# Scaling x by the FFN norm's factor on VectorE, and a new order of a pair's seven products, in a two-layer decoder trunk on one core

## The chip, the cores and the metric

The kernel runs on one core of one Trainium2 chip. The metric is device time in microseconds (us) for one execution; smaller is better. The median of three runs of the kernel before is 954.46 us (953.52 to 955.66).

## The reference

Two layers, 256 tokens, width 1024, float32. Each layer is an FFN, a token mixer (layer 0 stick-breaking attention, layer 1 latent attention), and another FFN, so there are four FFNs. Each of these is wrapped in a norm before and a norm after.

```python
def rms_norm(x, g):
    y = x * lax.rsqrt(jnp.mean(x * x, axis=-1, keepdims=True) + EPS)
    return y * g
def swiglu(x, w_in, w_out):
    gate, up = jnp.split(x @ w_in, 2, axis=-1)
    return (jax.nn.silu(gate) * up) @ w_out
...
f = swiglu(rms_norm(x, g[0]), ffn_w_in[i, 0], ffn_w_out[i, 0])
x = x + 0.5 * rms_norm(f, g[1])
```

## The kernel before, in words

The 256 tokens are two blocks of 128 (one token per partition). Every float32 product is made of three matmuls of a high and a low part: a weight piece (128 rows by 512 columns) is loaded, ScalarE rounds it to the high part (`split`, L368), VectorE subtracts to get the low part (L375), and TensorE runs hi*hi, hi*lo, lo*hi (`mm3`, L545). The pieces form one fixed stream. All operations are put in a list and a planner (`Plan.run`, L185) orders each engine's instructions ahead of time from assumed durations; an operation of class 0 goes ahead of the stream's work (class 1), and if a class 0 operation will be ready within `HOLD` us, the engine is left idle for it. On the chip each engine then runs its instructions strictly in that order.

**The norm ahead of an FFN** (`pre_norm`, L621, with `scaled=True`): for a block, ScalarE squares and sums the two halves of x (L609), VectorE adds the sums and eps into the mean square `msx` (L611, one number per token), GpSimd raises it to -0.5 with `half_neg` into `rpre` (L613), ScalarE scales the two halves of x by `rpre` (L634), TensorE transposes them in blocks of 128 (L551, 4 to a half), VectorE multiplies by the gain out of PSUM (L641). The result is split into high and low parts (L561 or L567, and L581), and these are the FFN's operands. This is done for both blocks, one after the other, while TensorE works on what it can.

**A pair** is 512 columns of gate and of up for both blocks at once, by seven 512-wide products in place of eight (`pair_product`, L769): the weights' quarters "11", "12", "21", "22" are combined by sums (`add_pair`, L416), some on VectorE (L434), some by a DMA that GpSimd issues and that adds on arrival (L437; which of them, `SUMS` tells). Each product is 4 pieces, so 12 matmuls. `STEPS` names the products in order: products 1, 6, 7 and 4 accumulate in one PSUM bank Z, 5 and 3 in a bank W, 2 in a bank Y. After products 1, 5 and 6 ScalarE copies the bank as it then stands to SBUF (`keep`, L759); the next product in the same bank can't write before the copy has been made. After 6 VectorE forms `up0` = W - m6 (L762), and then the hidden values of block 0.

`FFN_ORDERS` sets the order of the FFN's work: `s0.3` is the fourth product of pair 0, `i2` a plain tile of 256 columns, `o` and `t` rows of the second weight matrix. There are three pairs (s0, s1, s2). In pair 0 the products `s0.4` and `s0.5` follow one another directly; with `STEPS` = "1253674" these are 6 and 7.

Of the kernel before, what the change touches and what calls it, by code (L numbers as in the profile page):

```python
# [39 lines left out]
NEG = -(2.0 ** 100)  # L40


LEADS = [14, 12, 13, 17, 13, 7]
CAPS = [28, 27, 24, 26, 25, 26]
RESERVE = [4, 6, 2, 4, 3, 6]
AHEAD = 8
# [1 line left out]
ADD_US = 8.0  # L48
RSLOTS = 66
WSLOTS = 27  # L50
HOLD = 0.26
STOCK = 6
X1_AT = 1
WARM_A = 4
# [2 lines left out]


PAIR = 512
STEPS = "1253674"  # L60
SUMS = ["4", "124", "1"]
FFN_ORDERS = [
    ("s0.0 i0 i1 s0.1 s0.2 o0 o1 s0.3 s0.4 s0.5 i2 s0.6 s1.0 t0.0 s1.1 s1.2 t0.1 t0.2 s1.3 s1.4 i3 t0.3 s1.5 "
     "o2 s1.6 s2.0 s2.1 t1.0 t1.1 s2.2 t1.2 s2.3 s2.4 o3 s2.5 t1.3 s2.6 t2.0 i4 t2.1 t2.2 t2.3 o4"),
] * 4

# [40 lines left out]


class Op:
    __slots__ = ("eng", "us", "fn", "cls", "deps", "users", "wait", "bufs", "ready", "end", "table", "blk", "piece", "alt", "phase", "debt", "first", "lat", "size")  # L110


class Plan:
# [12 lines left out]
    def op(self, eng, us, fn, r=(), w=(), cls=0, after=(), table=None, blk=None, piece=None):  # L126
        o = Op()
        o.eng, o.us, o.fn, o.cls, o.table, o.blk, o.piece = eng, us, fn, cls, table, blk, piece
        o.alt = {}
        deps = set(after)  # L130
        bufs = {}
        for b, p in r:
            deps.update(b.wr.get(p, ()))
            b.rd.setdefault(p, []).append(o)
            bufs[id(b)] = b
        for b, p in w:
            deps.update(b.wr.get(p, ()))
            deps.update(b.rd.get(p, ()))
            b.wr[p] = [o]
            b.rd[p] = []  # L140
            bufs[id(b)] = b
        deps.discard(o)
        o.deps = list(deps)
        o.users = []
        o.wait = len(o.deps)
        o.bufs = list(bufs.values())
        o.ready, o.end = 0.0, None
        o.debt = 0
        o.first = None
        o.lat = 2.0 if eng == "dma" else 0.0  # L150
        o.size = 0
        for b in o.bufs:
            b.left += 1
        for d in o.deps:
            d.users.append(o)
        self.ops.append(o)
        return o
# [27 lines left out]
    def run(self):  # L185
        engines = ("pe", "act", "dve", "pool", "dma")
        at = dict.fromkeys(engines, 0.0)
        known = {e: [] for e in engines}

        def know(o):  # L190
            for e in (o.eng, *o.alt):
                known[e].append(o)

        for o in self.ops:
            if o.wait == 0:
                know(o)
        table = None
        left = len(self.ops)
        while left:
            best = None  # L200
            for e in engines:
                if not known[e]:
                    continue
                cand = []
                for o in known[e]:
                    if o.first is not None and (
                            o.first - self.split_pos >= AHEAD or
                            len(self.free["w"]) < KEEP):
                        continue
                    if o.debt > 0 and (self.held >= CAPS[o.phase] or  # L210
                                       len(self.free["r"]) - self.debt < 2 + RESERVE[o.phase]):
                        continue
                    cand.append((max(o.ready, self.slots_ready(o), self.bank_ready(o, e), at[e]), o))
                if not cand:
                    continue
                t = min(c[0] for c in cand)
                if t < math.inf and (best is None or t < best[0]):
                    best = (t, e, cand)
            assert best is not None, (at, self.held, self.pos, self.split_pos,
                                      {e: [(o.ready, o.cls, [b.tag for b in o.bufs]) for o in k[:6]] for e, k in known.items()},  # L220
                                      {t_: len(f) for t_, f in self.free.items()})
            t, e, cand = best
            now = [(o.cls, w, o) for w, o in cand if w <= t]
            if e == "pe":
                side = [c for c in now if c[0] == 0]
                if side:
                    o = min(side, key=lambda c: c[1])[2]
                else:
                    lead = self.pos[0] - self.pos[1]
                    by = {c[2].blk[0]: c[2] for c in now}  # L230
                    o = by[0] if 0 in by and (1 not in by or lead < LEADS[by[0].phase]) else by[1]
            else:
                o = min(now, key=lambda c: (c[0], c[1]))[2]
                if o.cls > 0 and (o.piece is None or self.split_pos - self.pos[0] >= STOCK):
                    soon = [w for w, q in cand if q.cls == 0 and t < w < t + HOLD]
                    if soon:
                        at[e] = min(soon)
                        continue
            us, fn = (o.us, o.fn) if e == o.eng else o.alt[e]
            if o.table is not None and o.table != table:  # L240
                self.set_table(o.table)
                table = o.table
                us += 1.3
            for b in o.bufs:
                if b.tile is None:
                    f = self.free[b.tag]
                    s_ = min(x for x in f)
                    f.remove(s_)
                    b.slot = s_[1]
                    b.tile = self.tiles[b.tag][b.slot]  # L250
            fn()
            at[e] = t + us
            o.end = t + us + o.lat
            if o.size:
                at["dma"] = max(at["dma"], t) + o.size / 180e3
            if o.piece is not None:
                if e == "act":
                    self.held += 1
                    self.split_pos = o.piece + 1
                elif e == "pe":  # L260
                    for q in o.blk:
                        self.pos[q] = o.piece + 1
                    if 1 in o.blk:
                        self.held -= 1
            self.debt += o.debt
            for b in o.bufs:
                b.touch[e] = o.end
                b.left -= 1
                b.end = max(b.end, o.end)
                if b.left == 0 and b.slot is not None:  # L270
                    self.free[b.tag].append((b.end + CROSS, b.slot))
            for q in (o.eng, *o.alt):
                known[q].remove(o)
            left -= 1
            for u in o.users:
                u.ready = max(u.ready, at[e] if u.eng == e and not u.alt else o.end + CROSS)
                u.wait -= 1
                if u.wait == 0:
                    know(u)
        return max(at.values())  # L280
# [11 lines left out]
def trunk(ctx: ExitStack, tc: tile.TileContext, x, positions, norm_g, ffn_w_in, ffn_w_out,  # L292
# [313 lines left out]
    def rstd(srcs, ss, ms, r, scale, eps, cls=0):  # L606

        for h, (src, rd) in enumerate(srcs):
            op("act", act_us(512, 1), lambda src=src, h=h: nc.scalar.activation(  # L609
                junk[:], src(), AF.Square, scale=scale, accum_out=ss[:, h:h + 1]), r=rd, w=[(ss, h)], cls=cls)  # L610
        op("dve", 0.13, lambda: nc.vector.tensor_scalar(ms[:], ss[:, 0:1], ss[:, 1:2], eps, op0=ALU.add, op1=ALU.add),  # L611
           r=[(ss, 0), (ss, 1)], w=[(ms, 0)])
        op("pool", 0.46, lambda: nc.gpsimd.tensor_tensor(out=r[:], in0=ms[:], in1=half_neg[:], op=ALU.pow),  # L613
           r=[(ms, 0)], w=[(r, 0)])

    def stats(b, cls):
        k = blocks[b]
        rstd([(lambda h=h: xt[b][h][:], [(xt[b][h], 0)]) for h in range(2)], k.ss2, k.ms2, k.rpre,
             1.0 / math.sqrt(D), EPS, cls)

    def pre_norm(b, l, i, scaled=False):  # L621

# [1 line left out]
        k = blocks[b]  # L624
        gi = (l * 6 + i) * KC
        k.xh, k.xl, k.y = [Buf("r"), Buf("r")], [Buf("r"), Buf("r")], [Buf("w"), Buf("w")]
        if scaled:
            stats(b, 0)
        for h in range(2):
            y, tr = k.y[h], Buf("bank")  # L630
            xs = xt[b][h]
            if scaled:
                xs = Buf("w")
                op("act", act_us(512, 1), lambda h=h, xs=xs: nc.scalar.activation(  # L634
                    xs[:], xt[b][h][:], AF.Copy, scale=k.rpre[:]), r=[(xt[b][h], 0), (k.rpre, 0)], w=[(xs, 0)])

            def turn(xs=xs, tr=tr):
                for c in range(4):
# [130 lines left out]
    def pair_product(l, f, p, step, st):  # L769
# [18 lines left out]
            vec512(st[nm], o, st[x], how)  # L788
        if q in "156":
            keep("m" + q)  # L790
            if q == "6":
                st["up0"] = Buf("w")
                vec512(st["up0"], st["W"], st["m6"], ALU.subtract)
                pair_hidden(0, p, st["gate0"], 1.0, st["up0"])
        elif q == "2":
            combine("gate0", "m1", ALU.add)
        elif q == "7":
            combine("up1", "m5", ALU.subtract)
        elif q == "4":
            pair_hidden(1, p, o, -1.0, st["up1"])  # L800

    def pair_hidden(b, p, gate, sign, up):
        h, hid = Buf("w"), Buf("w")
# [541 lines left out]
```

## Time and profile before

| | |
|---|---|
| runs, median of 3 | 954.46 us |
| the profiled execution, its own time | 953.05 us |
| its span, first to last instruction | 951.3 us |
| mean granted TensorE clock | 0.997 |
| ScalarE busy | 663.5 us (70%) |
| GpSimd busy | 104.3 us (11%) |

The span is what the views divide; 1.75 us of the execution's own time lie around it. Engines are PE (TensorE), PEld (its weight loads), DVE (VectorE), ACT (ScalarE), POOL (GpSimd). A wait is idle time of an engine just before an instruction, put down to the instruction that ended it.

### The profile page before, as it was taken

How to read it: one execution, taken by the hardware profiler on the slowest of the kernel's cores; microseconds unless marked ns; L12 is line 12 of the kernel's file. 1: busy time of each engine (PE TensorE's matmuls, PEld its weight loads, DVE VectorE, ACT ScalarE, POOL GpSimd, SP SyncE). 2: the span in 40 equal slices, each digit the busy share in tenths (PEclk: the TensorE clock that was granted, in tenths of full speed). 3: DMA queues.
4: the chain of work that ended last, by engine and by line, in shares of the span. 5: the costliest groups of instructions: out<-in, count | busy, mean ns of one | idle time of the engine just before them, and what ended most of it. 6: DMA issues, size and time to landing. Idle time of an engine off the chain costs nothing. (4 is left out here: it accounts for less than half of the span.)

```text
span 951.3 us, 14520 instructions
## 1 busy us (share of the span) xinstructions
PE 927.6 (98%) x4431; PEld 769.5 (81%) x4431; DVE 816.4 (86%) x1495; ACT 663.5 (70%) x1368; POOL 104.3 (11%) x155
## 2 busy tenths in 40 slices
PE   6999999999999899999999999999999999999997
PEld 4878888888888787888887878888898888788885
DVE  6999889877788898889978988797799999879982
ACT  8856767558798775767676666674689967576751
POOL 2013010000000112210001121100201000221000
PEclk9999999999999999999999999999999999999999
DMA  9799979834453369996933899778233255999731
GB/s 308 245 262 268 291 223 300 271 122 134 135 173 113 107 209 247 271 290 217 355 98 115 217 274 302 221 240 283 80 101 102 65 188 178 259 251 296 243 114 45
DMA packets 132462, 195.34 MB, mean 205 GB/s; under 512 B 12224, under 2 KB 63776, under 8 KB 132384
## 3 DMA queue, kind: packets, MB, share of 16 engines
q1 hardware_dynamic: 120752, 173.39, 54.9%
q0 software_dynamic: 11520, 20.98, 13.3%
q8 instruction: 35, 0.57, 0.2%
q14 instruction: 43, 0.35, 0.1%
q10 hardware_dynamic: 112, 0.05, 0.0%
HBM read 193.32 MB, written 1.05 MB: 204 GB/s over the span
## 5 line engine op out<-in xcount | busy, mean ns | idle before, releaser
L543 PE MATMUL bank<-r,r 128*128 128x512 f32 (+4 forms) x3936 | 890.1, 383 | 4.3 <-ACT w L759 3.4
L543 PEld LDWEIGHTS bank<-r,r 128*128 128x128 f32 (+1 forms) x3936 | 711.0, 188 | 141.4 <-ACT w L759 5.1
L375 DVE TENSOR_TENSOR r<-w,r 128x512 fp32r<-128x512 f32 (+2 forms) x772 | 485.7, 681 | 25.7 <-ACT r L368 20.9
L368 ACT CAST r<-w 128x512 fp32r<-128x512 f32 (+2 forms) x772 | 428.1, 617 | 79.1 <-DVE w L434 38.5
L437 POOL DMA_DIRECT2D w<-in_ffn_w_in_dram x80 | 70.9, 1140 | 339.9 <-DVE r L375 197.2
L561 ACT CAST r<-bank 128x256 fp32r<-128x256 f32 (+5 forms) x142 | 60.3, 440 | 44.6 <-PE bank L551 38.1
L581 DVE TENSOR_TENSOR r<-bank,r 128x256 fp32r<-128x256 f32 (+5 forms) x142 | 70.3, 503 | 15.6 <-ACT r L561 13.7
L434 DVE TENSOR_TENSOR w<-w,w 128x512 f32<-128x512 f32 x112 | 72.9, 683 | 0.0
L551 PE MATMUL bank<-ident,w 128*128 128x128 f32 (+1 forms) x390 | 62.3, 280 | 10.3 <-ACT w L634 9.3
L551 PEld LDWEIGHTS bank<-ident,w 128*128 128x128 f32 (+1 forms) x390 | 48.1, 140 | 26.5 <-ACT w L634 12.5
L715 ACT ACTIVATE w<-bank 128x256 f32<-128x256 f32 x40 | 15.3, 382 | 53.0 <-PE bank L543 52.9
L613 POOL TENSOR_TENSOR rpost<-ms,half_neg 128x1 f32<-128x1 f32 x12 | 6.6, 551 | 392.7 <-DVE ms L611 392.7
L759 ACT COPY w<-bank 128x512 f32<-128x512 f32 x36 | 21.1, 586 | 24.7 <-PE bank L543 24.2
L717 DVE TENSOR_TENSOR w<-bank,w 128x256 f32<-128x256 f32 x40 | 16.9, 421 | 23.0 <-ACT w L715 22.3
L762 DVE TENSOR_TENSOR w<-bank,w 128x512 f32<-128x512 f32 x36 | 24.8, 689 | 12.0 <-ACT w L759 7.8
L581 DVE TENSOR_TENSOR r<-w,r 128x512 fp32r<-128x512 f32 x48 | 32.4, 686 | 1.4 <-ACT r L576 0.4
L609 ACT ACTIVATE junk<-bank 128x512 bf16<-128x512 f32 x24 | 14.3, 596 | 18.3 <-PE bank L543 17.9
L660 DVE TENSOR_TENSOR w<-bank,w 128x512 f32<-128x512 f32 x24 | 16.4, 684 | 11.7 <-ACT junk L609 11.4
L762 DVE TENSOR_TENSOR w<-w,w 128x512 f32<-128x512 f32 x24 | 16.6, 692 | 8.8 <-ACT w L766 8.3
L641 DVE TENSOR_TENSOR w<-bank,gT 128x512 f32<-128x512 f32 x24 | 16.2, 685 | 5.7 <-PE bank L551 5.4
L766 ACT ACTIVATE w<-bank 128x512 f32<-128x512 f32 x12 | 7.2, 598 | 16.6 <-PE bank L543 10.3
L613 POOL TENSOR_TENSOR rpre<-msx,half_neg 128x1 f32<-128x1 f32 x12 | 13.5, 1122 | 45.0 <-DVE msx L611 32.0
(97 smaller groups left out, 331.7 us busy)
## 6 DMA issues: line engine op xcount, KB each, us to landing
w<-in_ffn_w_in_dram SPq DMA_DIRECT2D x368, 256.0 KB, 4.8
w<-in_ffn_w_out_dram SPq DMA_DIRECT2D x176, 256.0 KB, 5.2
w<-in_ffn_w_in_dram POOLq DMA_DIRECT2D x80, 256.0 KB, 7.4
w<-in_sb_w_in_dram SPq DMA_DIRECT2D x48, 256.0 KB, 5.2
w<-in_sb_w_out_dram SPq DMA_DIRECT2D x16, 256.0 KB, 3.6
w<-in_mla_w_out_dram SPq DMA_DIRECT2D x16, 256.0 KB, 3.1
w<-in_norm_g_dram SPq DMA_DIRECT2D x12, 256.0 KB, 4.2
w<-in_mla_w_in_dram SPq DMA_DIRECT2D x8, 208.0 KB, 4.7
```

The costliest lines, as they stand in the source:

```text
L368: h = op("act", act_us(n), lambda: nc.scalar.copy(pc.hi[:, :n], raw[:, :n]), r=[(raw, 0)], w=[(pc.hi, 0)], cls=1, after=splits[-1:], piece=i)
L375: nc.vector.tensor_tensor(out=pc.lo[:, :n], in0=raw[:, :n], in1=pc.hi[:, :n].bitcast(F32), op=ALU.subtract)
L434: op("dve", dve_us(PAIR), lambda d=d, t=t: nc.vector.tensor_add(out=d[:], in0=d[:], in1=t[:]), r=[(d, 0), (t, 0)], w=[(d, 0)], cls=1)
L437: o = op("pool", 0.9, lambda d=d, k=k: nc.gpsimd.dma_start(d[:], source(src, k), accum_op=ALU.add), r=[(d, 0)], w=[(d, 0)], cls=1)
L543: nc.tensor.matmul(o, a, b, start=start, stop=stop, skip_group_check=True)
L551: nc.tensor.transpose(o, i, ident[:])
L561: nc.scalar.copy(dst(), src())
L581: nc.vector.tensor_tensor(out=dst(), in0=src(), in1=hi().bitcast(F32), op=ALU.subtract)
L613: op("pool", 0.46, lambda: nc.gpsimd.tensor_tensor(out=r[:], in0=ms[:], in1=half_neg[:], op=ALU.pow), r=[(ms, 0)], w=[(r, 0)])
L717: op("dve", dve_us(FT), lambda: nc.vector.tensor_mul(out=hid[:, FT:], in0=o[:, FT:], in1=hid[:, 0:FT]), r=[(o, 0), (hid, 0)], w=[(hid, 1)])
L759: op("act", act_us(512), lambda: nc.scalar.copy(dst[:], src[:]), r=r, w=w)
L762: op("dve", dve_us(512), lambda: nc.vector.tensor_tensor(out=dst[:], in0=x[:], in1=y[:], op=o), r=[(x, 0), (y, 0)], w=[(dst, 0)])
```

## The change

The scaling of x by `rpre` moves from ScalarE to VectorE. Through a new field `then` of an operation the planner lets VectorE take nothing else between `msx` and the first scaling, nor between the first and the second. The products of a pair are made in the order 1, 2, 5, 6, 3, 7, 4; `up0` and what follows from it are made when 2, 3 and 6 are all done. In `FFN_ORDERS` the piece `t0.1` moves ahead of the second pair's second product. `HOLD` goes from 0.26 to 0.116, and one entry of `LEADS` (by how many pieces block 0 may be ahead of block 1, here in the second FFN) from 13 to 14.

```diff
-LEADS = [14, 12, 13, 17, 13, 7]
+LEADS = [14, 12, 14, 17, 13, 7]
...
-HOLD = 0.26
+HOLD = 0.116
...
-STEPS = "1253674"
+STEPS = "1256374"
...
-    ("s0.0 i0 i1 s0.1 s0.2 o0 o1 s0.3 s0.4 s0.5 i2 s0.6 s1.0 t0.0 s1.1 s1.2 t0.1 t0.2 s1.3 s1.4 i3 t0.3 s1.5 "
+    ("s0.0 i0 i1 s0.1 s0.2 o0 o1 s0.3 s0.4 s0.5 i2 s0.6 s1.0 t0.0 t0.1 s1.1 s1.2 t0.2 s1.3 s1.4 i3 t0.3 s1.5 "
...
+        only = {}
...
                 for o in known[e]:
+                    if only.get(e) not in (None, o):
+                        continue
...
             fn()
+            only[e] = o.then
...
-        if scaled:
-            stats(b, 0)
+        prev = stats(b, 0) if scaled else None
...
-                op("act", act_us(512, 1), lambda h=h, xs=xs: nc.scalar.activation(
-                    xs[:], xt[b][h][:], AF.Copy, scale=k.rpre[:]), r=[(xt[b][h], 0), (k.rpre, 0)], w=[(xs, 0)])
+                prev.then = op("dve", dve_fast_us(512) + 0.06, lambda h=h, xs=xs: nc.vector.tensor_scalar(
+                    xs[:], xt[b][h][:], k.rpre[:], None, op0=ALU.mult), r=[(xt[b][h], 0), (k.rpre, 0)], w=[(xs, 0)])
+                prev = prev.then
...
             keep("m" + q)
-            if q == "6":
-                st["up0"] = Buf("w")
-                vec512(st["up0"], st["W"], st["m6"], ALU.subtract)
-                pair_hidden(0, p, st["gate0"], 1.0, st["up0"])
...
+        done = STEPS[:step + 1]
+        if q in "236" and all(c in done for c in "236"):
+            st["up0"] = Buf("w")
+            vec512(st["up0"], st["W"], st["m6"], ALU.subtract)
+            pair_hidden(0, p, st["gate0"], 1.0, st["up0"])
```

VectorE in the third FFN, second block, before (w, r are SBUF buffers, x_193 the block's x; line 375 is a low part of the stream):

```order
L663 SCALAR_TENSOR_TENSOR x_193<-w_133,rpost_205,x_193 128x512
L434 TENSOR_TENSOR w_148<-w_148,w_136 128x512
L375 TENSOR_TENSOR r_110<-w_137,r_123 128x512
L611 TENSOR_SCALAR msx_207<-ssx_206 128x1
L375 TENSOR_TENSOR r_75<-w_134,r_105 128x512
L375 TENSOR_TENSOR r_63<-w_135,r_109 128x512
L375 TENSOR_TENSOR r_94<-w_141,r_111 128x512
L375 TENSOR_TENSOR r_96<-w_145,r_113 128x512
L375 TENSOR_TENSOR r_114<-w_153,r_68 128x512
L641 TENSOR_TENSOR w_137<-bank_158,gT 128x512
L641 TENSOR_TENSOR w_134<-bank_159,gT 128x512
```

The same place of the change, where lines stand 5 to 8 lower (L641 is now the scaling, L649 the gain, L439 a weight sum, L380 the low part):

```order
L671 SCALAR_TENSOR_TENSOR x_193<-w_145,rpost_205,x_193 128x512
L439 TENSOR_TENSOR w_135<-w_135,w_150 128x512
L380 TENSOR_TENSOR r_117<-w_128,r_104 128x512
L616 TENSOR_SCALAR msx_207<-ssx_206 128x1
L641 TENSOR_SCALAR w_144<-x_193,rpre_208 128x512
L641 TENSOR_SCALAR w_136<-x_193,rpre_208 128x512
L439 TENSOR_TENSOR w_131<-w_131,w_137 128x512
L649 TENSOR_TENSOR w_146<-bank_157,gT 128x512
L649 TENSOR_TENSOR w_153<-bank_160,gT 128x512
```

Five low parts stood between mean square and gain; now the two scalings and one weight sum stand there.

TensorE in the first FFN, pair 0, before: the last matmuls of product 6 and the first of product 7 (bank_160 is Z):

```order
L543 MATMUL bank_160<-r_107,r_103 128x512
L543 MATMUL bank_160<-r_84,r_103 128x512
L543 MATMUL bank_160<-r_107,r_120 128x512
L543 MATMUL bank_160<-r_109,r_88 128x512
L543 MATMUL bank_160<-r_87,r_88 128x512
L543 MATMUL bank_160<-r_109,r_102 128x512
```

The change, at the end of product 6:

```order
L548 MATMUL bank_160<-r_99,r_112 128x512
L548 MATMUL bank_160<-r_105,r_112 128x512
L548 MATMUL bank_160<-r_99,r_125 128x512
L548 MATMUL bank_156<-r_101,r_126 128x512
L548 MATMUL bank_156<-r_107,r_126 128x512
L548 MATMUL bank_156<-r_101,r_88 128x512
```

Product 3 in the other bank (bank_156, W) now follows product 6; product 7 comes 12 matmuls later.

## Rows read from the trace of the kernel before

**Rows 1.** The page's part 1: busy us of each engine, share of the span, instructions.
```profile
PE 927.6 (98%) x4431; PEld 769.5 (81%) x4431; DVE 816.4 (86%) x1495; ACT 663.5 (70%) x1368; POOL 104.3 (11%) x155
```

**Rows 2.** Waits of PE: line waited for, us in total, times, longest us.
```profile
PE bank L551 <- ACT w L634: 9.3, 4, 3.9
PE bank L543 <- ACT w L759: 3.4, 4, 1.3
PE bank L543 <- DVE r L375: 0.7, 2, 0.5
```

**Rows 3.** Timeline, third FFN, second block: start us, us, engine, line, form, count [idle before].
```profile
502.84 0.20 DVE L611 TENSOR_SCALAR msx<-ssx 128x1 f32<-128x1 f32 x1
502.96 3.09 DVE L375 TENSOR_TENSOR r<-w,r 128x512 fp32r<-128x512 f32 x5
503.19 3.27 POOL L613 TENSOR_TENSOR rpre<-msx,half_neg 128x1 f32<-128x1 f32 x1 [2.92 <-DVE msx L611]
507.27 1.62 PE L551 MATMUL bank<-ident,w 128*128 128x128 f32 x8 [2.10 <-ACT w L634]
507.96 0.69 DVE L641 TENSOR_TENSOR w<-bank,gT 128x512 f32<-128x512 f32 x1 [1.91 <-PE bank L551]
508.54 5.02 PE L543 MATMUL bank<-r,r 128*128 128x512 f32 x15
```

**Rows 4.** Timeline, second FFN: first block's factor, then the second block.
```profile
307.99 0.55 POOL L613 TENSOR_TENSOR rpre<-msx,half_neg 128x1 f32<-128x1 f32 x1 [3.81 <-DVE msx L611]
320.46 3.27 POOL L613 TENSOR_TENSOR rpre<-msx,half_neg 128x1 f32<-128x1 f32 x1 [2.92 <-DVE msx L611]
324.54 1.27 PE L551 MATMUL bank<-ident,w 128*128 128x128 f32 x8 [2.41 <-ACT w L634]
325.23 1.30 DVE L641 TENSOR_TENSOR w<-bank,gT 128x512 f32<-128x512 f32 x2 [1.91 <-PE bank L551]
325.56 2.77 PE L543 MATMUL bank<-r,r 128*128 128x512 f32 x11
```

**Rows 5.** Windows in the third FFN: us, PE busy, PEclk, DMA share, GB/s.
```profile
508.50:510.00 1.50, 1.50 (x6) 0.50 0.04 8
510.00:512.00 2.00, 2.00 (x7) 0.64 0.40 125
```

**Rows 6.** Timeline of the program's start, first block, and PE's first wait on VectorE.
```profile
5.77 0.56 POOL L613 TENSOR_TENSOR rpre<-msx,half_neg 128x1 f32<-128x1 f32 x1 [2.12 <-DVE msx L611]
7.52 0.72 ACT L634 ACTIVATE w<-x,rpre 128x512 f32<-128x512 f32 x1
8.29 1.12 PE L551 MATMUL bank<-ident,w 128*128 128x128 f32 x4 [3.93 <-ACT w L634]
9.45 0.69 DVE L641 TENSOR_TENSOR w<-bank,gT 128x512 f32<-128x512 f32 x1 [1.11 <-PE bank L551]
16.14 0.96 PE L543 MATMUL bank<-r,r 128*128 128x512 f32 x3 [0.49 <-DVE r L375]
```

**Rows 7.** Line L759 (copies of products): who waited, us and times.
```profile
  PE bank L543: 3.4, 4
```

**Rows 8.** VectorE's groups by shape: busy us, mean ns, idle before.
```profile
L375 DVE TENSOR_TENSOR r<-w,r 128x512 fp32r<-128x512 f32 x756 | 477.8, 683 | 25.7 <-ACT r L368 20.9 <-issue 1.8 <-PE bank L543 1.4
L567 DVE CAST r<-w 128x512 fp32r<-128x512 f32 x7 | 3.0, 427 | 0.2
L583 DVE SCALAR_TENSOR_TENSOR r<-bank,rpre,r 128x512 fp32r<-128x512 f32 x4 | 3.0, 748 | 0.1
```

**Rows 9.** Timeline, fourth FFN, second block.
```profile
770.21 3.09 DVE L375 TENSOR_TENSOR r<-w,r 128x512 fp32r<-128x512 f32 x5
770.43 0.86 POOL L613 TENSOR_TENSOR rpre<-msx,half_neg 128x1 f32<-128x1 f32 x1 [3.08 <-DVE msx L611]
```

**Rows 10.** Line L437 (accumulating DMAs), from issue to landing.
```profile
DMA to landing us min/median/max: 3.9/7.4/11.4
```

**Rows 11.** Chain that ended last, one long piece of PE: start us, us, count.
```profile
571.37 23.17 PE bank L543 x102
```

More of the change, by code (lines that the diff above doesn't have):

```diff
@@ L109 @@
 class Op:
-    __slots__ = ("eng", "us", "fn", "cls", "deps", "users", "wait", "bufs", "ready", "end", "table", "blk", "piece", "alt", "phase", "debt", "first", "lat", "size")
+    __slots__ = ("eng", "us", "fn", "cls", "deps", "users", "wait", "bufs", "ready", "end", "table", "blk", "piece", "alt", "phase", "debt", "first", "lat", "size", "then")
 class Plan:
@@ L151, in op @@
         o.size = 0
+        o.then = None
         for b in o.bufs:
@@ L610, in rstd @@
                 junk[:], src(), AF.Square, scale=scale, accum_out=ss[:, h:h + 1]), r=rd, w=[(ss, h)], cls=cls)
-        op("dve", 0.13, lambda: nc.vector.tensor_scalar(ms[:], ss[:, 0:1], ss[:, 1:2], eps, op0=ALU.add, op1=ALU.add),
-           r=[(ss, 0), (ss, 1)], w=[(ms, 0)])
+        o = op("dve", 0.13, lambda: nc.vector.tensor_scalar(ms[:], ss[:, 0:1], ss[:, 1:2], eps, op0=ALU.add, op1=ALU.add),
+               r=[(ss, 0), (ss, 1)], w=[(ms, 0)])
         op("pool", 0.46, lambda: nc.gpsimd.tensor_tensor(out=r[:], in0=ms[:], in1=half_neg[:], op=ALU.pow),
            r=[(ms, 0)], w=[(r, 0)])
+        return o
     def stats(b, cls):
         k = blocks[b]
-        rstd([(lambda h=h: xt[b][h][:], [(xt[b][h], 0)]) for h in range(2)], k.ss2, k.ms2, k.rpre,
-             1.0 / math.sqrt(D), EPS, cls)
+        return rstd([(lambda h=h: xt[b][h][:], [(xt[b][h], 0)]) for h in range(2)], k.ss2, k.ms2, k.rpre,
+                    1.0 / math.sqrt(D), EPS, cls)
     def pre_norm(b, l, i, scaled=False):
```

## The prediction

> **What bounds the kernel now.** Read first the busy times [rows 1]: TensorE works 927.6 of 951.3 us. No change of this kind makes its 4431 matmuls fewer, so all that can be won is in the 23.7 us in which TensorE stands, and in matmuls that run at a lower clock. VectorE comes next with 816.4 us: it is not the bound, but it is near enough that work put on it must be watched. So the second view is the list of TensorE's waits [rows 2]. Three lines matter: 9.3 us in four waits for transposes whose input, the scaled x, ScalarE had not made (L634); 3.4 us in four waits for ScalarE's copy of a product (L759); and only 0.7 us for low parts from VectorE (L375).
>
> Where are the 9.3 us? Two of the four waits lie at the program's start, the largest 3.93 us [rows 6]; the other two are 2.10 us in the third FFN [rows 3] and 2.41 us in the second [rows 4], each at the second block's norm. There the timeline shows the cause ahead of ScalarE: GpSimd's power on one number per token took 3.27 us, where the same instruction took 0.55 us at the first block of the second FFN [rows 4]. In the third FFN it began at 503.19 and ended at 506.46; VectorE meanwhile ran five low parts back to back, from 502.96 to 506.05 [rows 3]. GpSimd came through 0.4 us after VectorE stopped. In the fourth FFN the same pattern cost little: 0.86 us, under a run of five [rows 9]. So the delay is real but comes at some places only.
>
> The wait of 2.10 us has an after-effect: from 508.5 to 510 us TensorE was granted 0.50 of its clock and from 510 to 512 us a mean of 0.64 [rows 5], and fifteen matmuls took 5.02 us [rows 3]. That is the lower of its two levels (1.2 GHz in place of 2.4) after a stretch in which it had stood. After the 2.41 us wait eleven matmuls took 2.77 us [rows 4], so there it cost next to nothing.
>
> **The change part by part.** *The power and the scaling.* With VectorE idle between mean square and scaling, I take 0.55 us for the power [rows 4]. The scaling is a new form on VectorE. Below it is bounded by a cast of the same size from SBUF to SBUF, 0.427 us; above by the form that takes a per-token factor and a second tensor, 0.748 us [rows 8]. It has one tensor input like the cast, and the per-token factor costs 748 - 683 = 65 ns against the plain two-input form [rows 8]; I take 0.49 us. In the third FFN the scaled x is then there at 503.19 + 0.55 + 0.49 = 504.2, and TensorE ran dry only at 507.27 - 2.10 = 505.2 [rows 3]. In the second FFN: 320.46 + 1.04 = 321.5 against 324.54 - 2.41 = 322.1 [rows 4]; with 0.748 us it is still 321.8. Both waits go whole: 4.5 us. With the wait goes the low clock: 1.5 x 0.50 + 2.0 x 0.36 = 1.5 us [rows 5].
>
> What it costs: VectorE gets 16 scalings, 16 x 0.49 = 7.9 us (6.8 to 12.0 by the bounds), and eight holes from the end of the mean square (503.04) to the scaling (503.74), 0.7 us each [rows 3]. These lie beside TensorE's work as long as VectorE's low parts are ahead of their matmuls. At the two places above VectorE stood idle for 1.91 us anyway, waiting for the transposes [rows 3, 4]; there hole and scalings fit into it. What is behind VectorE's wait on its queue is low parts and weight sums, and TensorE waits for those 0.7 us in the whole kernel [rows 2]. ScalarE sheds its 16 scalings; it has slack, so that is worth nothing by itself. The first scaling of the kernel can begin at 5.77 + 0.56 = 6.33 in place of 7.52, as ScalarE was busy with something else [rows 6].
>
> *The start.* The transposes come some 1.4 us earlier, and VectorE, which stood for 1.11 us ahead of its gain at 9.45, starts earlier too [rows 6]. But the first dense matmuls wait for VectorE's low parts at 16.14 [rows 6], and VectorE gets four scalings and a hole in this stretch, 4 x 0.49 + 0.7 = 2.7 us. Ends: 1.4 us won, or 2.7 - 1.4 = 1.3 us lost. I take 0.
>
> *The order of products.* In pair 0, 7 came right behind 6 in the same bank and had to wait for the copy: 3.4 us in four waits, one per FFN [rows 2, 7]. Now product 3, in another bank, stands between. It takes 12 matmuls of 23.17 / 102 = 0.227 us [rows 11], 2.7 us, and covers the copy, for which TensorE waited 1.3 us at most [rows 2]. All 3.4 us go. Next in line is `up0` after product 3 on VectorE, whose transposes come only nine matmuls into product 7: 2.0 us against two VectorE instructions of 0.68 [rows 8]. I count nothing for it.
>
> *The rest.* `t0.1` earlier and 14 in `LEADS` only move TensorE's work. A smaller `HOLD` lets a low part or a cast slip in ahead of an urgent operation, at most one of 0.68 us [rows 8] at a time. The planner's tables all shift a little, so I add as much new waiting as VectorE causes today, 0.7 us [rows 2].
>
> Sum against the profiled execution: 953.05 - 4.5 - 1.5 - 3.4 + 0.7 = 944.35 us. The median of the runs is 954.46, 1.41 us above that execution; on its scale I predict **945.8 us**, about 0.9% faster. A measurement of this kernel can tell some 0.2% (1.9 us) from no change.
>
> **The rivals.** *The power stays slow (6%).* If one VectorE instruction at most holds GpSimd up, 0.68 + 0.55 = 1.23 us of the 3.27 us is explained, and the other 2.04 us has a cause that an idle VectorE does not remove. For it speaks the 0.86 us under a run of five [rows 9]; against it, that both long powers ended 0.4 us after VectorE's run did [rows 3]. Then each wait shrinks only by 0.68 and by the quicker scaling, some 0.9 us, and the low clock stays: 945.8 + 2.7 + 1.5 = 950.0 us. The Trainium skill says it this way (SBUF — State Buffer, section "Who interferes with whom"): a VectorE instruction with two SBUF inputs and a GpSimd instruction that reads SBUF share a port, and the one that comes second is blocked until the first has ended. By that sentence alone the rival holds; the trace here shows a run of five holding it all the way.
>
> *The accumulating DMAs come late (12%).* In pair 1 the weights of product 6 are those of 5, onto which a DMA adds, and it can start only when 5 has been split. Eight pieces of the stream stood between 5 and 6; now two, and TensorE wants 6 one product, 2.7 us, earlier [rows 11]. The DMA takes 7.4 us, at times 11.4 [rows 10]. ScalarE would stand at that split with all else behind it. Where the stock of pieces is small (first and fourth FFN) that could cost up to 2.7 us each: 945.8 + 5.5 = 951.3 us. Against it: TensorE waits for low parts only twice today [rows 2].
>
> *VectorE becomes the bound (9%), the case that ends slower.* Scalings and holes of one FFN take 4 x 0.49 + 2 x 0.7 = 3.4 us of VectorE. They decide from the point where its low parts are less than that ahead of TensorE. At the second and third FFN the 1.91 us of idle [rows 3, 4] speak against it; the start does wait for VectorE [rows 6], and in the fourth FFN it ran without a gap [rows 9]. If those two are exposed, 945.8 + 6.8 = 952.6 us; if all four, 945.8 + 13.6 = 959.4 us, slower than before.
>
> *A stall elsewhere by the planner's new tables (4%)*, mostly in the attention layers, 3 to 10 us.
>
> **How the numbers follow.** The forecast has 69%, with its own range of 942.5 to 948: below, 1.4 us at the start, no new waits (0.7) and 1.2 us of small waits that go along; above, 1.3 us lost at the start and 0.9 us of new waits. The range of 942.5 to 951.3 takes in the first two rivals and leaves out VectorE as the bound and the unforeseen stall. Faster by over 0.2% (below 952.6): 69 + 6 + 12, and a little of the rest, 88%; within 0.2%: 6%; slower: 6%.
>
> **What would show it.** Right: all eight powers ahead of an FFN at about 0.55 us; the scaling at 0.43 to 0.5 us; in TensorE's waits neither the 2 us waits of second and third FFN nor any for L759's line; full clock through the third FFN's start; TensorE's busy time lower by about 1.5 us, its idle by about 8. Wrong: a power of over 1 us with VectorE idle; new waits of TensorE on low parts of over 3 us; ScalarE standing on an accumulating DMA in pair 1 while TensorE waits too.

## The result and the profile after

The changed kernel takes 941.54 us (median of 4 runs, 940.56 to 942.32), the kernel before 954.09 us beside it: ratio 0.9865, 95% interval 0.9848 to 0.9882. That is 12.5 us less. The forecast was 945.8 us with a range from 942.5: the direction was right, the gain a third too small, and the result lies 1 us outside the range. The profiled execution after has a span of 938.8 us and took 940.56 us, against 953.05 us before, so the two traces hold 12.5 us between them too.

The page's busy times after, answering to [rows 1]:

```profile
PE 924.5 (98%) x4431; PEld 768.8 (82%) x4431; DVE 811.4 (86%) x1504; ACT 653.9 (70%) x1360; POOL 97.7 (10%) x155
```

TensorE is 3.1 us less busy with the same 4431 matmuls (about 1.5 forecast), and stands 14.3 us in place of 23.7 (about 8 less forecast). VectorE has 16 scalings more and yet is busy for no longer than before, 811.4 against 816.4 us: it did not become the bound. TensorE's waits after (columns as in [rows 2]):

```profile
PE bank L556 <- DVE w L641: 2.7, 2, 2.4
PE bank L548 <- DVE r L380: 1.7, 2, 0.9
PE bank L548 <- DVE w L342: 1.5, 1, 1.5
```

The two lines of [rows 2] that the change was aimed at, 9.3 us and 3.4 us, are gone. What is left for the scaled x is the program's start, 2.4 us, and 0.4 us for the second block there. The low parts cost 1.7 us where they cost 0.7, also at the start. The third line is the program's first matmul; it waited 1.5 us in the kernel before too.

GpSimd's powers, by form, before and then after (minimum, median and maximum in ns; x12 are the eight norms ahead of an FFN and the four ahead of a mixer):

```profile
L613 POOL TENSOR_TENSOR rpre<-msx,half_neg x12: 547/768/3268, 5.8 to 770.4; 128x1 f32<-128x1 f32 x12
```

```profile
L618 POOL TENSOR_TENSOR rpre<-msx,half_neg x12: 547/548/863, 5.7 to 759.4; 128x1 f32<-128x1 f32 x12
```

The one of 863 ns stands ahead of a mixer. The third FFN's second block after, where [rows 3] showed 3.27 us and a wait of 2.10 us (timeline; start us, us, engine, line, form, count, idle before):

```profile
496.83 0.55 POOL L618 TENSOR_TENSOR rpre<-msx,half_neg 128x1 f32<-128x1 f32 x1 [3.41 <-DVE msx L616]
497.42 0.88 DVE L641 TENSOR_SCALAR w<-x,rpre 128x512 f32<-128x512 f32 x2 [0.73 <-POOL rpre L618]
...
498.30 1.03 PE L556 MATMUL bank<-ident,w 128*128 128x128 f32 x8
...
499.09 3.67 PE L548 MATMUL bank<-r,r 128*128 128x512 f32 x15
```

Power 0.55 us, hole 0.73 us, TensorE goes from the stream to the transposes and back without a gap. The fifteen matmuls that took 5.02 us in [rows 3] take 3.67 us, and the granted clock is full (windows, columns as in [rows 5] with all engines ahead of the clock):

```profile
495.00:500.00 5.00, 5.00 (x28) 4.23 (x27) 4.22 (x9) 2.99 (x9) 0.55 (x1) 1.00 0.45 160
500.00:505.00 5.00, 5.00 (x25) 4.09 (x24) 5.00 (x10) 3.33 (x8) 0.00 (x0) 1.00 0.31 103
```

VectorE's scaling, by shape, between the bounds of [rows 8]:

```profile
L641 DVE TENSOR_SCALAR w<-x,rpre 128x512 f32<-128x512 f32 x16 | 7.1, 487 | 5.7 <-POOL rpre L618 5.7
```

487 ns, where 490 was taken; and 5.7 us of holes for the eight, 0.7 each, as forecast.

**Where the 12.5 us come from.** Both kernels run 4431 matmuls. The start of the n-th matmul in the trace before, less its start in the trace after, tells what has been won up to there:

| stretch | won, us | what I had taken |
|---|---|---|
| program's start | 1.05 | 0 |
| second FFN's norm | 2.75 | 2.41 |
| third FFN's norm with the lower clock | 4.1 | 2.10 + 1.5 |
| the four copy waits | 4.0 | 3.4 |
| all else | 0.6 | -0.7 |
| sum | 12.5 | 8.7 |

Of the 1.05 us at the start 0.64 us stand at the fiftieth matmul; the rest is a wait of 0.21 us at 28.52 us for the hidden values of a plain tile (L717), which is gone. Of the 2.75 us 0.2 us are won at the first block's norm, where I had expected nothing.

### The profile page after: what moved, and what is told of

Its sections match the earlier page's. It is cut to its first block, busy times and chain, and to the rows that moved or that the text cites. A ratio compares the mean times of both kernels' runs of the same rounds, so it can differ in the third digit from the quotient of the medians.

```text
span 938.8 us, 14416 instructions
## 1 busy us (share of the span) xinstructions
PE 924.5 (98%) x4431; PEld 768.8 (82%) x4431; DVE 811.4 (86%) x1504; ACT 653.9 (70%) x1360; POOL 97.7 (10%) x155
## 3 DMA queue, kind: packets, MB, share of 16 engines
HBM read 193.32 MB, written 1.05 MB: 207 GB/s over the span
## 4 chain that ended last, share of the span: by engine, by line
PE 94%; DVE 3%; issue 1%; ACT 1%; POOL 1%; DMA 0%; POOLq 0%; DVEq 0%; ACTq 0%
PE bank L548 90%; PE bank L556 5%; DVE r L586 1%; DVE r L380 1%; DMA w<-in_ffn_w_in_dram 0%; DVE mx L1247 0%; POOL crs L1169 0%; DVE x L671 0%; DVE w L649 0%; DVE w L641 0%; ACT w L947 0%; ACT w L950 0%; POOL rpre L618 0%; ACT r L373 0%; DVE r L588 0%
## 5 line engine op out<-in xcount | busy, mean ns | idle before, releaser
L380 DVE TENSOR_TENSOR r<-w,r 128x512 fp32r<-128x512 f32 (+2 forms) x772 | 485.3, 683 | 31.7 <-ACT r L373 30.5
L373 ACT CAST r<-w 128x512 fp32r<-128x512 f32 (+2 forms) x772 | 426.1, 618 | 75.6 <-DVE w L439 46.5
L566 ACT CAST r<-bank 128x256 fp32r<-128x256 f32 (+5 forms) x142 | 60.5, 441 | 45.7 <-PE bank L556 39.8
L586 DVE TENSOR_TENSOR r<-bank,r 128x256 fp32r<-128x256 f32 (+5 forms) x142 | 70.0, 501 | 12.1 <-ACT r L566 10.2
L439 DVE TENSOR_TENSOR w<-w,w 128x512 f32<-128x512 f32 x112 | 73.3, 684 | 0.1
L770 DVE TENSOR_TENSOR w<-bank,w 128x512 f32<-128x512 f32 x36 | 24.7, 687 | 17.3 <-PE bank L548 10.9
L586 DVE TENSOR_TENSOR r<-w,r 128x512 fp32r<-128x512 f32 x48 | 31.9, 686 | 1.5 <-PE bank L548 0.7
L725 DVE TENSOR_TENSOR w<-bank,w 128x256 f32<-128x256 f32 x40 | 16.8, 420 | 12.8 <-ACT w L723 12.8
L614 ACT ACTIVATE junk<-bank 128x512 bf16<-128x512 f32 x24 | 14.3, 598 | 18.4 <-PE bank L548 17.9
L770 DVE TENSOR_TENSOR w<-w,w 128x512 f32<-128x512 f32 x24 | 16.6, 690 | 6.2 <-ACT w L774 5.7
L566 ACT CAST r<-w 128x512 fp32r<-128x512 f32 x23 | 13.7, 618 | 5.8 <-DVE w L649 5.7
L671 DVE SCALAR_TENSOR_TENSOR x<-w,rpost,x 128x512 f32<-128x512 f32 x24 | 17.0, 746 | 0.4
```

The lines of the kernel that those rows point to most:

```text
L373: h = op("act", act_us(n), lambda: nc.scalar.copy(pc.hi[:, :n], raw[:, :n]), r=[(raw, 0)], w=[(pc.hi, 0)], cls=1, after=splits[-1:], piece=i)
L380: nc.vector.tensor_tensor(out=pc.lo[:, :n], in0=raw[:, :n], in1=pc.hi[:, :n].bitcast(F32), op=ALU.subtract)
L439: op("dve", dve_us(PAIR), lambda d=d, t=t: nc.vector.tensor_add(out=d[:], in0=d[:], in1=t[:]), r=[(d, 0), (t, 0)], w=[(d, 0)], cls=1)
L566: nc.scalar.copy(dst(), src())
L586: nc.vector.tensor_tensor(out=dst(), in0=src(), in1=hi().bitcast(F32), op=ALU.subtract)
L671: op("dve", dve_us(512) + 0.06, lambda h=h, t=t: nc.vector.scalar_tensor_tensor(xt[b][h][:], t[:], k.rpost[:], xt[b][h][:], op0=ALU.mult, ...
```

## Experiments

The edits are shown against the changed kernel.

**The scaling alone.** STEPS, FFN_ORDERS, HOLD and LEADS as before.

```diff
-LEADS = [14, 12, 14, 17, 13, 7]
+LEADS = [14, 12, 13, 17, 13, 7]
...
-HOLD = 0.116
+HOLD = 0.26
...
-STEPS = "1256374"
+STEPS = "1253674"
...
```

> Only the scaling on VectorE with nothing between mean square and scaling; order of products, HOLD, LEADS and t0.1 as before. My theory (the long powers at the second and third FFN were VectorE's runs holding GpSimd, and each wait of TensorE costs its idle time plus about 0.16 us of modelled matmul end): all eight powers at 0.55 us, the two waits of over 2 us and the low clock gone, the start about 1 us earlier, the four waits for the product's copy still there (3.4 us): 954.1 - 4.6 - 1.4 - 1.0 = about 947. Rival (the planner's tables carry the gain): under 3 us gained, 951 or more.

Measured: 948.39 us, ratio 0.9944 (0.9922 to 0.9967). All eight powers ahead of an FFN took 0.55 to 0.57 us and both 2 us waits went; the copy waits stayed:

```profile
PE bank L556 <- DVE w L641: 4.1, 3, 2.4
PE bank L548 <- ACT w L767: 2.8, 4, 0.7
PE bank L548 <- DVE r L380: 1.5, 1, 1.5
```

The traced execution is the slowest of the five (951.06 us; the fastest took 946.53). What it lost is at its start: 3.05 us behind the kernel before at the hundredth matmul. TensorE stood 1.50 us for a low part until 16.66 us, and its matmuls, at half speed since the program began, stayed there until 22.7 us, though the windows print a granted clock of 1.00. The groups of TensorE from 16.66 to 22.6 us, and from 23 to 36 us (busy us, mean ns of one; 0.45 and 0.23 us of busy time a matmul):

```profile
L548 PE MATMUL bank<-r,r 128*128 128x512 f32 x14 | 6.3, 635 | 1.5 <-DVE r L380 1.5
```

```profile
L548 PE MATMUL bank<-r,r 128*128 128x512 f32 x58 | 13.6, 391 | 0.0
```

So the scaling on VectorE does fix the norms by itself, and the start is where it can cost. My zero for the start was a sum of two things that need not cancel.

**The order of products alone.** The scaling on ScalarE, HOLD and LEADS as before; `t0.1` stays at its new place, other than the expectation has it.

> Only the new order of the products (1256374); scaling on ScalarE, HOLD, LEADS and t0.1 as before. My theory: the four waits for the copy go, 4 x (idle + 0.16) = 4.0 us, nothing new comes: about 950; a wait for a long power may still come or go by chance. Rival (the accumulating DMAs come late): ScalarE stands over 2 us on one in pair 1 and TensorE waits; gain under 2 us, 952 or more.

Measured: 947.84 us, 0.9931 (0.9909 to 0.9954). No copy wait is left, and the two powers of 3.27 us are there as before:

```profile
PE bank L556 <- ACT w L641: 9.6, 4, 4.2
PE bank L548 <- DVE r L380: 0.7, 2, 0.5
```

The rival of late accumulating DMAs falls here: TensorE waits for no weights, and ScalarE stands at the splits for loads of the FFN's first weights for 22.9 us, 3.8 at most, where it was 23.9 and 3.5. The order is worth more than its 3.4 us. One reason is in how a wait is printed. TensorE ahead of one copy wait, in the kernel before:

```profile
360.70 4.92 PE L543 MATMUL bank<-r,r 128*128 128x512 f32 x21
366.29 0.97 PE L543 MATMUL bank<-r,r 128*128 128x512 f32 x3 [0.68 <-ACT w L759]
```

At 0.227 us a matmul [rows 11] the next one could have begun 21 steps after 360.70, at 365.47; it began at 366.29, 0.82 us late, and the row says 0.68. The idle time is counted from the end of the last matmul, which stands 0.38 us behind its start, while the next may begin after 0.227. Each wait thus costs about 0.15 us more than its row. The Trainium skill has this in "Perfetto Trace Analysis", section "Summary: the profiler window per engine type": TensorE's reported end is an estimate. The trace agrees, and here that is four times 0.15 us for the copies. The order also removed TensorE's wait of 0.4 us for `up0`, which I had left standing. Together these make 4.6 of the 4.8 us between the two traced executions (953.05 and 948.27 us). The medians lie 6.0 us apart, more than I expected with the undercount already taken in; where that further gain comes from is not shown.

**HOLD and LEADS alone.**

> Only HOLD 0.116 and the one entry of LEADS. My theory: 954.1 within 1.5 us, but for waits on long powers that come or go with VectorE's new order. Rival (the planner's tables carry the part of the gain that I did not foresee): 951.5 or less, with waits on long powers as before.

Measured: 951.89 us, 0.9979 (0.9965 to 0.9993). That lies between the two expectations. The traced execution is the fastest of the ten (949.77 us). The four copy waits stay (3.6 us in all). The power of 3.27 us is gone from the second and third FFN, where all four took 0.86 to 0.87 us, but it has moved to the fourth (GpSimd's timeline):

```profile
753.15 1.53 POOL L613 TENSOR_TENSOR rpre<-msx,half_neg 128x1 f32<-128x1 f32 x1 [3.30 <-DVE msx L611]
...
765.74 3.27 POOL L613 TENSOR_TENSOR rpre<-msx,half_neg 128x1 f32<-128x1 f32 x1 [2.99 <-DVE msx L611]
```

By the matmul starts this version is 6.0 us ahead behind the third FFN's norm and 6.5 us before the fourth FFN, and gives 3.3 us of it back by the end of the fourth FFN's norm. Another table shifted which norm is hit.

The three parts alone give 5.5, 6.0 and 2.0 us, 13.5 in all, against 12.5 together. The sum comes near, but the parts aren't independent: alone, HOLD with the entry of LEADS is worth a long power at one place; the run with HOLD taken back out shows what it is worth beside the scaling. No run takes LEADS or `t0.1` by itself.

**The order taken back out of the whole change**, with `t0.1` at its old place in FFN_ORDERS.

```diff
-STEPS = "1256374"
+STEPS = "1253674"
...
```

> The whole change with the old order of a pair (STEPS 1253674 and the attention order that goes with it). Theory (the four copy waits are all that the order is worth, by the steps of the matmul starts 4.0 us of them): four waits for the copy again, 945 to 946.5 us. Rival (with the scaling on VectorE the products come at other moments and the copy waits are partly gone): 942 to 944 us.

Measured: 946.43 us, 0.9922 (0.9902 to 0.9943), 4.9 us slower than the whole change. Four copy waits are back (2.8 us in the list of waits, 0.84 to 0.89 us each by the matmul starts). The rival falls. But the copies make only 3.4 us; the largest part of the rest stands in the fourth FFN, where TensorE waits 0.83 us for a plain tile's hidden values (L725) and 0.41 us for L770, the line of `up0` and of the hidden values made from it.

**HOLD taken back out of the whole change.**

```diff
-HOLD = 0.116
+HOLD = 0.26
```

> The whole change with HOLD alone back at 0.26. Theory (the smaller HOLD lets VectorE make the first low part ahead of the scaled x's remainders, so that TensorE does not stand long at 15 us; I had taken the start as worth nothing): a wait for a low part of about 1.5 us at the start, TensorE at its lower clock for longer there, 943 to 945 us. Rival (HOLD is worth nothing beside the rest): 941 to 942 us.

Measured: 945.59 us, 0.9927 (0.9903 to 0.9951), 4.0 us slower than the whole change and a little above what the theory had. VectorE at the start, and the windows that follow (columns as above):

```profile
12.33 1.28 DVE L649 TENSOR_TENSOR w<-bank,gT 128x512 f32<-128x512 f32 x2
13.84 1.29 DVE L586 TENSOR_TENSOR r<-w,r 128x512 fp32r<-128x512 f32 x2 [0.23 <-ACT r L566]
15.05 3.10 DVE L380 TENSOR_TENSOR r<-w,r 128x512 fp32r<-128x512 f32 x5
```

```profile
15.60:19.00 3.40, 3.21 (x8) 2.53 (x9) 3.40 (x7) 3.02 (x6) 0.00 (x0) 0.50 1.12 325
19.00:22.00 3.00, 3.00 (x15) 2.44 (x14) 3.00 (x6) 2.60 (x6) 0.00 (x0) 1.00 0.99 332
```

VectorE stands 0.23 us for the remainders, the low parts of the scaled x (L586), and makes them first; the low part that TensorE wants next comes at 15.05 us. TensorE stands 2.30 us for it, and its granted clock is 0.50, the lower of its two levels, until 19 us. By the fiftieth matmul 1.9 us are lost. In the whole change the first low part goes ahead, at 13.51, and TensorE waits 0.89 us and 0.84 us:

```profile
14.24 0.97 PE L548 MATMUL bank<-r,r 128*128 128x512 f32 x3 [0.89 <-DVE r L380]
16.05 4.14 PE L548 MATMUL bank<-r,r 128*128 128x512 f32 x17 [0.84 <-DVE r L380]
```

The rest comes in the fourth FFN, where places at 761 to 764 us and at 849 us cost up to 0.9 us each by the matmul starts. So HOLD, which I had dismissed as "one of 0.68 us at a time", is worth as much as a norm once the scaling is on VectorE.

**HOLD lower still, 0.06.**

> The whole change with HOLD at 0.06 in place of 0.116: a version that might beat both. Theory (HOLD pays by the first low part going ahead of the scaled x's remainders at the start, which both values give): the start as in the whole change, 940.5 to 943 us. Rival (less is better all over, since every held instruction costs VectorE time): 939 us or less.

Measured: 944.98 us, 0.9905 (0.9889 to 0.9922), 3.4 us slower than the whole change. The start is as in the whole change (0.4 us behind at the fiftieth matmul); 2.1 us are lost at 700 to 704 us in the latent attention and 1.2 us about the fourth FFN's norms, where TensorE waits for remainders and high parts (L586, L566); the line of L380 is the two waits at the start:

```profile
PE bank L548 <- DVE r L380: 2.4, 2, 1.2
PE bank L548 <- DVE r L586: 1.7, 4, 0.6
PE bank L548 <- ACT r L566: 0.8, 1, 0.8
```

Both expectations missed: less is not better, and the start isn't all. 0.116 is the best of the three values tried.

**The whole change without the reservation.** `then` is not set, so the planner may put other work between mean square and scaling.

```diff
-                prev.then = op("dve", dve_fast_us(512) + 0.06, ...
+                op("dve", dve_fast_us(512) + 0.06, ...
```

> The whole change, but VectorE may do other work between mean square and scaling; the planner puts two instructions there, mostly low parts with two SBUF inputs. My theory: powers last up to 1.5 us where two low parts run (they end 0.4 us after the second), since VectorE then stops and waits for the power itself; TensorE waits under 1 us at each; 941.5 to 944. Rival (a shorter chain is what counts, and GpSimd is not held up by VectorE): all powers at 0.55 us, time as with the whole change within 0.5 us.

Measured: 941.52 us, 0.9872 (0.9853 to 0.9891): no difference from the whole change. At six of the eight norms one or two instructions with two SBUF inputs come there, and those powers take 0.86 to 1.53 us, yet none 3.27 (GpSimd's timeline in the second FFN):

```profile
305.28 0.86 POOL L618 TENSOR_TENSOR rpre<-msx,half_neg 128x1 f32<-128x1 f32 x1 [3.61 <-DVE msx L616]
...
317.78 1.47 POOL L618 TENSOR_TENSOR rpre<-msx,half_neg 128x1 f32<-128x1 f32 x1 [3.30 <-DVE msx L616]
```

With the scaling on VectorE's own queue, VectorE must stop and wait for the power, so its run of low parts ends there: the move bounds the delay even without the reservation. By the matmul starts this version is 1.0 us ahead of the whole change behind the start, where low parts use the hole, and gives 1.6 us back at the other three FFNs.

**An idle VectorE, and the scaling on ScalarE.** All else as in the whole change.

```diff
-                prev.then = op("dve", ... nc.vector.tensor_scalar(xs[:], xt[b][h][:], k.rpre[:], ...
+            prev.then = op("dve", 0.13, lambda: nc.vector.tensor_scalar(tick[:], k.rpre[:], 1.0, ...
+                op("act", act_us(512, 1), ... nc.scalar.activation(xs[:], xt[b][h][:], AF.Copy, scale=k.rpre[:]) ...
```

> The whole change, except that the 16 scalings stay on ScalarE and VectorE, which is kept empty until the power is done, does only a tiny multiplication there. Theory (what held the scalings up was the power, and the power was held up by VectorE's runs): all eight powers ahead of an FFN at 0.55 us as in the whole change, none of the 2 us waits for the transposes, 941.5 to 943.5 us. Rival (it is the move of the scaling to VectorE that pays, because ScalarE is late by itself): the powers are short and yet TensorE waits 1 us or more for ScalarE's scaling in some FFNs, 944 us or more.

Measured: 943.56 us, 0.9897 (0.9881 to 0.9913), at the upper end of what the theory had. The powers are 0.55 to 0.56 us at all eight norms. Of the 2.0 us to the whole change 1.0 us is lost at the start, where TensorE waits 3.6 us for ScalarE's scaling, the rest bit by bit at the other three FFNs, 0.4 us at most at one norm. What pays in the change is an idle VectorE beside the power; that VectorE then also does the scaling is worth the last 2 us.

**What of VectorE holds the power up.** Three runs put four instructions without use between mean square and scaling of each of the eight norms, and leave nothing out: additions of two SBUF tiles into one tile; maxima over one SBUF tile; and additions into four tiles.

```diff
+            fill = Buf("w")
+            for _ in range(4):
+                prev.then = op("dve", dve_us(512), ... tensor_tensor(out=fill[:], in0=xt[b][0][:], in1=xt[b][1][:], op=ALU.add) ...
+                prev = prev.then
```

> The whole change, with four additions of two SBUF tiles (128x512, 0.68 us each, the result is not used) put on VectorE between mean square and scaling at each of the eight norms; nothing is left out. Theory (a run of VectorE instructions with two SBUF inputs holds GpSimd's power up): powers at these norms of 0.86 us to 3.2 us, at least half of them over 1.4 us, and those end about 0.4 us after the end of an addition. Rival (something else made the powers slow): they stay at 0.55 us. Either way the scaling waits for the four additions, 2.7 us, of which TensorE had at most 1 us to spare: slower than the whole change by 10 to 20 us.

> As fill_two, with four maxima over one SBUF tile (128x512 in, 128x2 out, one SBUF input each; the result is not used) in the place of the additions. Theory: all eight powers at 0.55 us, though VectorE is as busy. Rival (any work of VectorE on SBUF holds GpSimd up): powers like those of fill_two. The time is about that of fill_two, as the scaling waits for the fill in both.

> As fill_two, with the four additions writing four different tiles, so that none waits for the one before it, as the low parts in the kernel before; nothing is left out. In the run with one tile the additions stood 0.035 us apart, and the power came through after the first, every time. Theory (a run without gaps can hold the power up to its end): at some of the eight norms a power of 1.4 us or more, of 2.6 us at most (four additions at a step of 0.6 us, less 0.2 us, and 0.41 us behind the last). Rival (one instruction at most holds it up, as the page on SBUF reads, and the 3.27 us of the kernel before had another cause): all eight at 0.86 to 0.94 us. The time: 949 to 953 us by either.

Measured: 951.54, 951.28 and 950.28 us (0.9986, 0.9974 and 0.9955; intervals 0.9973 to 0.9999, 0.9962 to 0.9985 and 0.9941 to 0.9969). The powers of the second FFN's two norms, first under the additions into one tile:

```profile
312.70 0.86 POOL L618 TENSOR_TENSOR rpre<-msx,half_neg 128x1 f32<-128x1 f32 x1 [3.61 <-DVE msx L616]
...
325.46 0.86 POOL L618 TENSOR_TENSOR rpre<-msx,half_neg 128x1 f32<-128x1 f32 x1 [3.30 <-DVE msx L616]
```

Under the maxima:

```profile
311.54 0.55 POOL L618 TENSOR_TENSOR rpre<-msx,half_neg 128x1 f32<-128x1 f32 x1 [3.61 <-DVE msx L616]
...
324.27 0.55 POOL L618 TENSOR_TENSOR rpre<-msx,half_neg 128x1 f32<-128x1 f32 x1 [3.31 <-DVE msx L616]
```

Under the additions into four tiles:

```profile
311.90 0.86 POOL L618 TENSOR_TENSOR rpre<-msx,half_neg 128x1 f32<-128x1 f32 x1 [3.61 <-DVE msx L616]
...
324.29 2.67 POOL L618 TENSOR_TENSOR rpre<-msx,half_neg 128x1 f32<-128x1 f32 x1 [3.31 <-DVE msx L616]
```

All eight powers under the maxima took 0.55 to 0.56 us, though a maximum (684 ns) keeps VectorE as busy as an addition (690 ns): it is not work as such that holds the power up. A maximum also writes less, 128x2 in place of 128x512, but that is not the difference either. The gain reads one tile from PSUM and one from SBUF and writes 128x512, and beside it a power ahead of a mixer took 0.55 us (timeline of the kernel before):

```profile
188.79 0.68 DVE L641 TENSOR_TENSOR w<-bank,gT 128x512 f32<-128x512 f32 x1
188.96 0.55 POOL L613 TENSOR_TENSOR rpre<-msx,half_neg 128x1 f32<-128x1 f32 x1 [2.38 <-DVE msx L611]
```

What is left of the difference between the maxima and the additions is the second SBUF input. It is not the only thing that holds a power up: a cast from SBUF to SBUF has one input, and the power beside it came late too (the same trace, first FFN, second block):

```profile
10.18 0.42 DVE L567 CAST r<-w 128x512 fp32r<-128x512 f32 x1
10.35 0.68 POOL L613 TENSOR_TENSOR rpre<-msx,half_neg 128x1 f32<-128x1 f32 x1 [1.85 <-DVE msx L611]
```

That power ended 0.42 us after the cast, and in the traces of the other runs twelve more powers beside such a cast ended 0.40 to 0.42 us after it.

Under additions into one tile, each of which starts 0.035 us after the one before it, all eight took 0.86 to 0.94 us: my expectation of longer ones missed, GpSimd came through after the first every time. Under additions into four tiles, each of which starts 0.08 us before the one ahead of it ends, five took 0.86 to 0.94 us and three 2.67 to 2.73 us, held to the end of the run and 0.41 us more, as in [rows 3, 4]. The Trainium skill ("SBUF — State Buffer", section "Who interferes with whom") says that a VectorE instruction with one SBUF input doesn't contend, outside the modes in which it takes both ports, and that one with two does: the maxima and the additions agree, and whether the cast ran in such a mode no trace shows. It has the loser blocked for one instruction; here that holds with a gap, and without one the loser was held for four or five at some places.

**A version meant to beat both:** the reservation left out at the first FFN alone.

```diff
+                if l:
+                    prev.then = o
```

> The whole change with the reservation (then) left out at the first FFN alone, so that low parts may go between mean square and scaling there, and kept at the other three: a version meant to beat both. In the run without any reservation the matmuls behind the start came 1.0 us earlier than in the whole change, and the other three FFNs gave 1.6 us back. Theory (the two are independent): 940.0 to 941.0 us. Rival (the order behind the start shifts with it and brings other waits): 941.5 us or more.

Measured: 940.58 us (940.38 to 940.85), ratio 0.9859 (0.9843 to 0.9876), as the theory had it. It is the fastest of all by the medians, but the intervals overlap, and 1.0 us is under the 0.2% that a measurement of this kernel can tell. The waits for low parts at the start are gone there (0.15 us left at 18.01).

## Why the prediction was wrong

- **Right: what held the scaling up.** The powers fell to 0.55 us, both 2 us waits went, and the runs with added instructions show the cause. "Both waits go whole: 4.5 us" and "with the wait goes the low clock: 1.5 us" came to 6.85 us in place of 6.0: 0.3 us by the undercount of an idle row at two waits, 0.2 us at the second FFN's first block, and some 0.3 us as the lower clock cost nearer 1.8 us (4.1 less 2.10 and 0.15) than 1.5. I had counted it from 508.5 us; the window ahead of that shows a mean clock of 0.82, another 1.3 x 0.18 = 0.2 us:

```profile
507.20:508.50 1.30, 1.23 (x8) 0.82 0.53 188
```

- **Right: the copy waits go, and product 3 covers them.** "All 3.4 us go" was 4.0 us, by the same undercount, four times.
- **Wrong: "I take 0" for the start.** It gave 1.05 us, 0.64 of them by the fiftieth matmul. In the whole change the bounds of +1.4 and -1.3 held, but where in them it comes out hangs on whether one low part goes ahead of the remainders, which HOLD decides: with HOLD at 0.26 it was 1.9 us less, a loss of 1.3 against the kernel before. With the scaling alone the traced execution lost 3.05 us, beyond the bounds, which had left out that its matmuls ran at half speed until 22.7 us. I had bounded the start by two sums of VectorE's time and taken the middle, without following TensorE's next low part through VectorE's new order.
- **Wrong: "I add as much new waiting as VectorE causes today, 0.7 us".** No new wait of over 0.2 us came beyond the start, and small old ones went, 0.6 us net, the wait for `up0` among them. This is the step that cost most, 1.3 us: a margin for the unforeseen written into the sum, where it belonged in the range. Without it the forecast would have been 945.1 us, with the measured size of the norms and the copies 943.7, and with the start 942.6.
- **Wrong: the range's lower end.** It took in the start and the small waits (each at its best), but no error in the terms that were read from rows, which came out 1.4 us too small together.
- **The rivals.** "The power stays slow" is refuted: an idle VectorE brings 0.55 us, whoever scales. Late accumulating DMAs didn't show in either run with the new order. VectorE as the bound didn't come at all with HOLD at 0.116, and came in part with 0.26: 4.0 us, at the start and in the fourth FFN, the two places that the rival named, though some of it was waits for ScalarE's parts (L566, L373).

## What to carry to other kernels

Price a stall of TensorE by the step from matmul to matmul, not by the idle time that the row shows, which left out 0.15 us at each here. When a small GpSimd instruction stands on the path, keep VectorE's two-input work, and its casts from SBUF to SBUF, away from it, or let VectorE itself wait for it, which bounds the delay. A margin for the unforeseen belongs in the range and not in the sum.

## What the hardware showed that was not expected

- GpSimd's power under back-to-back two-input instructions of VectorE ended 0.41 us after the first of them, after the second, or after all four or five (0.86, 1.47, 2.67 and 3.27 us), and which of these came differed between places with the same kind of run. With gaps of 0.035 us between them it was the first, in eight of eight. What decides it without gaps stays open.
- Of the waits of 2.1 to 2.4 us the lower clock followed some and not others. In the kernel before it came behind the 2.10 us wait of the third FFN and not the 2.41 us wait of the second [rows 4, 5]; with the new order alone it was the second's, 2.44 us (windows, columns as above), and not the third's, 2.09 us; with HOLD and LEADS alone the wait of 2.13 us in the fourth FFN had none behind it:

```profile
325.00:327.50 2.50, 2.50 (x10) 2.12 (x9) 2.14 (x4) 1.80 (x3) 0.00 (x0) 0.50 0.14 52
```

- At the program's start the matmuls ran at half speed until 11.9 us in the whole change, 13.1 us in the kernel before and 22.7 us with the scaling alone, while the profile prints 1.00 there; the duration of a matmul told it, the granted clock did not.
